# A hybrid decoder layer: dummy products at the start, copies of x moved, a bank and two products reordered

## The chip, the cores and the metric

The kernel runs on one core of a Trainium2 chip. The core has a matrix engine (TensorE, PE in the profile, with its weight loads as PEld), a vector engine (VectorE, DVE), a scalar engine (ScalarE, ACT), a general engine (GpSimd, POOL) and a synchronising engine (SyncE, SP) that here mainly issues DMAs. Each engine has its own queue of instructions, and they wait for each other by semaphores. The metric is the device time of one execution in microseconds; lower is better.

## What is computed

One layer of a decoder with 1024 positions and width 1024, in float32: a normalisation, one wide projection, two groups of heads side by side (differential softmax attention and chunked gated linear attention, GLA), an output projection, a second normalisation and the residual. Cut to what matters:

```python
def hybrid_layer(x, layer_idx, pre_g, post_g, w_in, w_gk_up, b_gk, ...):
    h = rms_norm(x, pre_g)
    z = jnp.einsum('bsd,de->bse', h, w_in)          # 1024 x 1024 by 1024 x 7184
    qa, ka, va, ga, qb, kb, vb, gb, gk_low = split_columns(z)
    ...
    oa = diff_attention(qa, ka, va, lam)            # 8 heads, causal
    oa = rms_norm(oa, subln_g) * (1.0 - lam_init)
    oa = oa * jax.nn.silu(ga)
    gk = jnp.einsum('bsr,re->bse', gk_low, w_gk_up) + b_gk
    log_a = jax.nn.log_sigmoid(gk) / 16.0
    ob = gla_chunked(qb, kb, vb, log_a)             # 4 heads
    ob = rms_norm(ob, gla_g) * jax.nn.silu(gb)
    y = jnp.einsum('bse,ed->bsd', jnp.concatenate([oa, ob], axis=-1), w_out)
    return x + rms_norm(y, post_g)
```

## The kernel before

Each float32 matrix product is made of three products in a reduced format: an operand is split into a high part (a cast, on ACT) and a low part (operand minus high part, on DVE), and high by high, high by low and low by high are added up in PSUM. All matmuls are issued at line 117 (`mm`) and all transposes at line 120 (`tr`), in the program's order on PE.

**The projection** is done by a seven-product scheme of the Strassen-Winograd kind over halves of positions and of the inner dimension. The columns of `w_in` are cut into units (`pairs`) of 256 columns; unit p and number n (1 to 7) name a product (p, n), which is 24 matmuls, 256 or 512 columns wide. The list `order` holds all products in the order in which PE runs them; `go(n)` issues the next n of them through `step`. Four units at the start, those for the values of GLA, are "wide" and share weights in twos: (0, n) and (1, n) use the same weight tiles. Numbers 1 and 2 are the first products of the left blocks h11 and h12, numbers 5, 6, 4 and 7 use the blocks s1, s2, h22 and s3, and number 3 uses s4.

**PSUM** has eight banks, handed out in turn from the list `free` (`take_bank`); a bank is put back by the Python code at once when its last reader is issued, so the next user waits for that reader by a semaphore. In `step`, number 1 opens a bank "x", 2 or 4 a bank "y", 5 a bank "z"; 6 and 7 add to "x" and 3 to "z". After 1, 6 and 7 ACT copies the running sum out (`snap`, line 427); `done` adds a copy to a bank on DVE (lines 403, 440) and the bank goes back.

**Weights.** `prepare(i)` makes the two weight tiles of `order[i]` ahead of its use: DVE forms differences in place where the scheme wants them (line 296), ACT casts the high part (line 315), DVE writes the low part (line 316). They lie in a ring of five buffers. The raw columns come by DMA into four buffers (`load_raw`, line 194); the first ten products use weights that are loaded early (`load_early`, line 236) for units 2, 3 and 4. The early tiles of unit 4 (128 wide) lie where one early tile of unit 2 was, so that their load waits until that one has been used.

**The start.** The first four tiles of x (128 positions each) are loaded, squared with a running sum on ACT (line 491), turned into a factor by `rstd` (lines 1480 to 1490) and scaled on DVE, first half, and POOL, second half (line 482). `first(0)` transposes the first half of the columns into four banks; `put` writes the blocks h11 (high on ACT, line 521, low on DVE, line 522). The product (0, 1) follows, then `first(1)` for h12, two more products, the normalisation of the tiles 4 to 7 in twos, one more product, and then four `blocks(j)`, with a product behind each. `blocks(j)` transposes two pieces of the other positions into two banks and makes h22, s1, s2 and s3 from them: evictions on ACT (lines 562 and 521), sums on DVE (lines 522, 565, 568, 569), and casts and low parts (lines 547 and 548). The block s4 follows (line 625).

**The low-rank part** of the gate (`low_rank`) loads small weights, splits them on DVE into `wl2` and `ku` (lines 647 to 656), then runs two groups of sixteen narrow products between those of the projection.

**The order of the other engines.** A scheduler in the framework sorts the instructions of ACT, DVE, POOL and SP by a timeline of its own, except those that the kernel pins with `keep_in_program_order`. The attention, GLA and output stages behind the projection have their own hand-written merge; the diff does not touch them, apart from six copies of 512 KB from x to the output (line 1275), onto which the last stage adds for the positions 512 to 1023 and 0 to 255. They stand in the program in the attention stage; the scheduler put them early in SP's queue.

Of the kernel before, what the change touches and what calls it, by code (L numbers as in the profile page):

```python
# [31 lines left out]
def hymba_kernel(  # L32
# [20 lines left out]
    nc = tc.nc  # L53
    act, dve, pool, pe, sp = nc.scalar, nc.vector, nc.gpsimd, nc.tensor, nc.sync

# [5 lines left out]


    const = ctx.enter_context(tc.tile_pool(name="const", bufs=1))
    pre_g = const.tile([P, KT], F32, name="pre_g")
    ident = const.tile([P, P], F32, name="ident")
    make_identity(nc, ident)
    eps_t = const.tile([P, 1], F32, name="eps_t")
    pool.memset(eps_t, EPS)
    ones = const.tile([P, P], F32R, name="ones")
    pool.memset(fp(ones), 1.0)  # L70

    NZ = 512
# [50 lines left out]

    edge = ctx.enter_context(tc.tile_pool(name="edge", bufs=1, side="right"))
    pool.memset(edge.tile([P, 120], F32, name="edge"), 0.0)
    hw = ctx.enter_context(tc.tile_pool(name="hw", bufs=1, side="right", reuse_waits="tile"))
    hpool_cm = tc.tile_pool(name="hpool", bufs=1, side="right")
# [89 lines left out]
    i = order.index((1, 4))  # L217
    order[i : i + 2] = order[i + 1], order[i]

    order += [(y, 1), (y, 2), (y - 1, 3), (y, 5), (z, 1), (z, 2), (z, 5), (y, 6), (z, 6), (y, 4)]  # L220
    order += [(y, 7), (z, 4), (z, 7), (y, 3), (z, 3)]
    LEAD = 8
    ws, ws_wide, early = {}, {}, {}

# [13 lines left out]
    def prepare(i):  # L238

        if i >= len(order) or i in ws:  # L240
            return
        if i < 4:

            act_ins, dve_ins = normed[0][:2]
            with tc.issue_after(act_ins.ins), tc.issue_after(dve_ins.ins):
                make_weights(i)
        else:
            make_weights(i)
# [70 lines left out]
    LEFT = {1: "h11", 2: "h12", 3: "s4", 4: "h22", 5: "s1", 6: "s2", 7: "s3"}  # L319
    NRING = 5  # L320

    def multiply(i, ps, start):
# [97 lines left out]
    def step(i):  # L420
# [22 lines left out]
        if n == 1:  # L443
            snap("s1", ps)
        elif n == 2:
            done(0, 0, ps, b["s1"])
            free.append(b["iy"])
        elif n == 6:
            snap("s2", ps)
        elif n == 7:  # L450
            snap("s3", ps)
            free.append(b["ix"])
            done(1, 1, b["z"], b["s3"])
            done(1, 0, b["y"], b["s3"])
            free.append(b["iy"])
        elif n == 3:
            done(0, 1, ps, b["s2"])
            free.append(b["iz"])
# [24 lines left out]

    norms, normed = {}, []

    def norm_x(*sts):
        n = len(sts)
        ssq = const.tile([P, 4, n], F32, tag=f"ssq{sts[0]}", name="ssq", bufs=1)
        for i, st in enumerate(sts):
            junk = hw.tile([P, D], F32, tag=("s2_hi0", "s2_lo0")[st % 2], name="junk")  # L490
            ins = act.activation(
                junk, xs[st], AF.Square, scale=D**-0.5, accum_out=ssq[:, 0, i : i + 1]
            )
            if n == 1:
                tc.keep_in_program_order(ins)
        pin = tc.keep_in_program_order if n == 1 else None
        normed[:] = [rstd(nc, ssq[:, :, :n], ssq[:, 0, :n], eps_t, pin)]
        for i, st in enumerate(sts):
            norms[st] = ssq[:, 1, i : i + 1]
            if n == 1:  # L500
                pin(scale_x(st, cols(0), dve))
            else:
# [9 lines left out]
    load_early(2)  # L512
    load_early(4)
    for st in range(4):
        norm_x(st)
# [13 lines left out]
    def first(h):  # L529

        ps = [take_bank([P, 512], "xT") for _ in range(HB)]
        for i in range(4):
            for j in range(HB):
                k = h * HB + j
                tr(ps[j][0][:, i * P : (i + 1) * P], xs[i][:, k * P : (k + 1) * P])
        hi, lo = H[("h11", "h12")[h]]
        for j in range(HB):
            put(ps[j][0], h * HB + j, (hi, lo), j)
            if h:
                act.activation(f1[h][:, j], ps[j][0], AF.Copy, scale=pre_g[:, h * HB + j : h * HB + j + 1])  # L540
# [39 lines left out]
    def wo_step(n):  # L580
# [8 lines left out]
        if n in (2, 4) and wo_todo:  # L589
# [3 lines left out]
            wo_open.append((e, dh, raw))  # L593

    def go(n):
        for _ in range(n):
            i = made[0]
            if i == len(order):
                return
# [8 lines left out]

    prepare(0)
    first(0)  # L610
    for i in range(1, 4):
        prepare(i)
    go(1)
    first(1)
    go(2)
    norm_x(4, 5)
    norm_x(6, 7)
    go(1)
    for j in range(HB):
        blocks(j)  # L620
        go(1)
    go(2)
# [11 lines left out]
    def low_rank():  # L634
# [21 lines left out]
        dve.tensor_tensor(up[96 : 96 + R], gk_up, fp(up[0:R]), ALU.subtract)  # L656
        go(2)
        for half in range(2):
# [51 lines left out]

    go(6)
    sp.dma_start(bgk, b_gk[0].rearrange("(t p) -> p t", p=P))
    low_rank()
# [5 lines left out]

    sp.dma_start(sub_g, attn_subln_g[0].rearrange("(p o) -> p o", o=1))  # L720
    dve.tensor_scalar(sub_g, sub_g, 1.0 - LAM_INIT, None, ALU.mult)
    sp.dma_start(gla_g, gla_norm_g[0].rearrange("(t p) -> p t", p=P))
    lam4 = t_c("lam4").rearrange("p (a b) -> p a b", b=128)[:, :, :64]
# [535 lines left out]
    def out_early():  # L1259
# [12 lines left out]
        for st in range(1, NT - 1):  # L1272
            part, nxt = nxt, mix(st + 1)
            rows = slice(ENDS[st - 1] * P, ENDS[st - 1] * P + P)
            sp.dma_start(out[0, rows, :], x[0, rows, :])
            for dh in range(2):
# [91 lines left out]

    LAST, ENDS = 2, [4, 5, 6, 7, 0, 1, 2, 3]

# [155 lines left out]
```

## Time and profile before

| | |
|---|---|
| time, median of 3 runs | 979.69 us (978.42 to 980.46) |
| the profiled execution | 979.08 us |
| its span, first to last instruction | 977.4 us |
| granted TensorE clock, mean over the span | 0.999 |
| DMA traffic | 220.45 MB, mean 226 GB/s |
| first matmul work | 7.21 us |
| the six copies of x, issued by SP from | 20.46 us |

The profile lists instructions by line of the kernel, engine, operation and tile. A row of the timeline begins with the start and the duration in us, then engine, line, operation, the tile written and those read, the shape, and how many instructions are merged (x16); in square brackets stands how long the engine had been idle before and what ended that. Matmuls are pipelined: the duration of one row reaches a little into the next. In the list of waits, a row has the waiting engine, tile and line, what it waited for, and us in total, number of waits, longest wait. In the chain of waits, a row has start, duration and what held the end of the execution at that time. In the list of DMA issues, the last figure is the median time in us from issue to landing.

### The profile page before, as it was taken

The page shows a single profiled execution, that of the slowest core. Times are in us where ns is not written, and L with a number is a line of the kernel's source. Part 1 is how long each engine was busy: PE and PEld are TensorE (multiplying, and loading weights), DVE is VectorE, ACT ScalarE, POOL GpSimd, SP SyncE. Part 2 cuts the span into 40 slices and gives each one's busy share as a digit, 9 for nine tenths or more (in the row PEclk, how much of TensorE's full clock was granted, in tenths as well). Part 3 has the DMA queues.
Part 4 walks back from the last instruction along what each step waited for, and adds up shares of the span by engine and source line. Part 5 has one row for each costly group of instructions (what it writes and reads, how often), then busy time and mean ns, then how long its engine had stood idle before and what let it go on. Part 6 is the DMA issues. An engine that isn't in the chain of part 4 may idle for free.

```text
span 977.4 us, 15766 instructions
## 1 busy us (share of the span) xinstructions
PE 956.7 (98%) x5338; PEld 830.4 (85%) x5338; DVE 735.4 (75%) x1452; ACT 600.5 (61%) x1164; POOL 142.9 (15%) x158
## 2 busy tenths in 40 slices
PE   5999999999999999999999999999999999999997
PEld 5998988888889998999888888878888888888785
DVE  6887597789866667686786876487888888898554
ACT  8742455487357455454665775366776687887773
POOL 4300000000000010000200002121322222443321
PEclk9999999999999999999999999999999999999999
DMA  9432446656774868897987866987656669994677
GB/s 345 151 110 91 139 135 205 231 179 225 238 247 162 264 187 286 254 294 229 293 259 243 273 202 191 407 269 272 197 186 228 240 199 344 340 294 105 151 208 147
DMA packets 152593, 220.45 MB, mean 226 GB/s; under 512 B 17104, under 2 KB 83664, under 8 KB 152416
## 3 DMA queue, kind: packets, MB, share of 16 engines
q1 hardware_dynamic: 146176, 203.71, 64.1%
q0 software_dynamic: 6336, 15.73, 7.0%
q8 instruction: 42, 0.69, 0.3%
q14 instruction: 39, 0.32, 0.1%
HBM read 133.93 MB, written 88.60 MB: 228 GB/s over the span
## 4 chain that ended last, share of the span: by engine, by line
PE 95%; DVE 2%; ACT 1%; DMA 1%; issue 1%; POOL 0%; SPq 0%; DVEq 0%; ACTq 0%; POOLq 0%
PE x L117 24%; PE y L117 15%; PE z L117 15%; PE ypart L117 13%; PE sc L117 7%; PE po L117 5%; PE yps L117 4%; PE wtr L120 3%; PE gpo L117 3%; PE kv L117 1%; PE gkl_ps L117 1%; PE pa L117 1%; DMA x<-in_x_dram 1%; PE xT L120 1%; DVE s_lo L548 0%
## 5 line engine op out<-in xcount | busy, mean ns | idle before, releaser
L315 ACT CAST w<-w_raw 128x512 fp32r<-128x512 f32 (+1 forms) x164 | 112.4, 688 | 94.7 <-PE y L117 44.1
L316 DVE TENSOR_TENSOR w<-w_raw,w 128x512 fp32r<-128x512 f32 (+1 forms) x164 | 126.7, 774 | 50.1 <-ACT w L315 43.3
L1049 ACT ACTIVATE p<-p,stt 128x896 f32<-128x896 f32 (+7 forms) x128 | 99.3, 777 | 36.7 <-DVE stt L1039 33.9
L427 ACT COPY s<-x 128x512 f32<-128x512 f32 x84 | 49.1, 585 | 84.4 <-PE x L117 84.3
L775 POOL TENSOR_SCALAR_AFFINE_SELECT gan<-gan 128x512 f32<-128x512 f32 x8 | 16.5, 2060 | 485.4 <-ACT gan L774 449.8
L296 DVE TENSOR_TENSOR w_raw<-w_raw 128x512 f32<-128x512 f32 (+1 forms) x96 | 75.9, 791 | 13.9 <-DMA w_raw<-in_w_in_dram 12.6
L1039 DVE CUSTOM_DVE_ANT_0 p<-sc,maskt 128x512 f32<-128x512 f32 (+3 forms) x128 | 74.3, 585 | 14.5 <-PE sc L117 13.3
L117 PE MATMUL ypart<-wo_hi,m_hi 128*128 128x512 f32 x192 | 79.5, 414 | 0.1
L117 PE MATMUL y<-h_hi,w 128*128 128x512 f32 x320 | 79.6, 391 | 0.0
L117 PE MATMUL z<-s_hi,w 128*128 128x512 f32 x320 | 79.6, 391 | 0.0
L117 PE MATMUL x<-s_hi,w 128*128 128x512 f32 x320 | 79.6, 391 | 0.0
L1055 POOL TENSOR_SCALAR p<-p,stt,lam 128x1024 f32<-128x1024 f32 (+3 forms) x64 | 56.2, 879 | 146.9 <-DVE stt L1054 141.9
L117 PE MATMUL ypart<-wo_hi,m_lo 128*128 128x512 f32 x192 | 75.5, 393 | 0.0
L117 PE MATMUL ypart<-wo_lo,m_hi 128*128 128x512 f32 x192 | 75.4, 393 | 0.0
L117 PE MATMUL sc<-k,q 128*128 128x512 f32 (+1 forms) x192 | 69.0, 363 | 1.3 <-DVE stt L1039 1.2
L117 PEld LDWEIGHTS x<-s_hi,w 128*128 128x128 f32 x320 | 59.7, 188 | 12.2
L117 PEld LDWEIGHTS y<-h_hi,w 128*128 128x128 f32 x320 | 59.6, 188 | 12.2
L117 PEld LDWEIGHTS z<-s_hi,w 128*128 128x128 f32 x320 | 59.5, 188 | 12.0
L117 PE MATMUL sc<-ks,q 128*128 128x512 f32 (+1 forms) x192 | 66.1, 347 | 0.0
L1097 ACT CAST wt_hi<-wtr 128x512 fp32r<-128x512 f32 (+1 forms) x80 | 42.7, 534 | 24.6 <-PE wtr L120 23.8
L1098 DVE TENSOR_TENSOR wt_lo<-wtr,wt_hi 128x512 fp32r<-128x512 f32 (+1 forms) x80 | 50.7, 633 | 8.6 <-ACT wt_hi L1097 8.0
L1058 DVE SCALAR_TENSOR_TENSOR p<-p,stt,p 128x1024 f32<-128x1024 f32 (+3 forms) x64 | 52.1, 814 | 4.1 <-POOL p L1055 3.9
(226 smaller groups left out, 2247.7 us busy)
## 6 DMA issues: line engine op xcount, KB each, us to landing
w_raw<-in_w_in_dram SPq DMA_DIRECT2D x56, 512.0 KB, 4.7
wo_raw<-in_w_out_dram SPq DMA_DIRECT2D x32, 256.0 KB, 3.0
wo_d<-wo_hi SPq DMA_DIRECT2D x32, 256.0 KB, 2.8
wo_d<-wo_raw SPq DMA_DIRECT2D x32, 256.0 KB, 3.8
q<-q_d SPq DMA_DIRECT2D x32, 256.0 KB, 4.7
k<-k_d SPq DMA_DIRECT2D x32, 256.0 KB, 5.7
ks<-k_d SPq DMA_DIRECT2D x64, 128.0 KB, 6.2
v<-v_d SPq DMA_DIRECT2D x16, 512.0 KB, 7.0
```

Of the source, the lines that this page charges most:

```text
L117: tc.keep_in_program_order(pe.matmul(*a, **k))
L120: tc.keep_in_program_order(pe.transpose(dst, src, ident))
L296: dve.tensor_tensor(dst, a, b, ALU.subtract)
L315: act.copy(w[0], src)
L316: dve.tensor_tensor(w[1], src, fp(w[0]), ALU.subtract)
L427: act.copy(b[k], ps)
L1039: ins = dve.tensor_tensor_reduce(p[:, a:e], sc[:, : e - a], maskt[:, NZ + P - (e - a) :] if last else maskt[:, : e - a], 1.0, 3e38 if i == ...
L1049: act.activation(p[:, :n], p[:, :n], AF.Exp, bias=st[:, m : m + 1], scale=-1.0, accum_out=st[:, 2 + m : 3 + m],)
L1055: pool.tensor_scalar(p1[:, :n], p1[:, :n], st[:, 5:6], lam, ALU.mult, ALU.mult)
L1058: dve.scalar_tensor_tensor(p0[:, :n], p0[:, :n], st[:, 4:5], p1[:, :n], ALU.mult, ALU.subtract)
L1097: act.copy(hi[:, :n], pt[:, :n])
L1098: dve.tensor_tensor(lo[:, :n], pt[:, :n], fp(hi[:, :n]), ALU.subtract)
```

## The change

- **Dummy products.** A tile `idle` of zeros is made on POOL, the tile `ones` and another memset are moved ahead of the identity. `spin(n)` issues n matmuls of 512 columns, `ones` by `idle`, which are added up in one tile in a bank that is free at the time; the result is read by nobody. 14 are put ahead of the transposes of `first(0)`, then 3, 7, 3 and 4 behind the transposes of its four tiles.
- **Copies of x.** The six copies leave the attention stage and are issued, pinned, ahead of the products with index 20, 24, 28, 32, 36 and 40 of `order`.
- **An early bank.** Ahead of the product behind the last `blocks(j)`, which is (3, 2), the second bank in the free list is moved to its front.
- **Two products' order.** (1, 4) is moved two places back instead of one, so (1, 7) comes before it; the sum that needs both 4 and 7 is taken behind the later of them.
- **The low-rank preparation** starts one product earlier (`go(5)` and `go(3)` in place of `go(6)` and `go(2)`), its matmuls stay in place.
- **Pinned order.** ACT, DVE and POOL are wrapped in a class that pins every instruction issued while a flag is set: from the first normalisation to the end of the second `put`. Within this stretch the weights of the first four products are now prepared ahead of `first(0)`, the normalisation of the tiles 4 to 7 and the product (0, 1) stand ahead of `first(1)`, and the weights with index 4 to 10 are made only behind the last pinned instructions. Three small loads are pinned where they stand in the program, later than the scheduler had put them.

In the built program the instructions of each engine differ in order up to about the second decay computation of the projection; behind that they stand as before. PE has 31 more matmuls.

```diff
-    act, dve, pool, pe, sp = nc.scalar, nc.vector, nc.gpsimd, nc.tensor, nc.sync
+    pe, sp = nc.tensor, nc.sync
+    pinned = [False]
+
+    class Queue:
...
+        def __getattr__(self, name):
+            op = getattr(self.engine, name)
+
+            def run(*a, **k):
+                ins = op(*a, **k)
+                if pinned[0]:
+                    tc.keep_in_program_order(ins)
+                    self.last = ins.ins
+                return ins
+
+            return run
+
+    act, dve, pool = Queue(nc.scalar), Queue(nc.vector), Queue(nc.gpsimd)
...
+    ones = const.tile([P, P], F32R, name="ones")
+    pool.memset(fp(ones), 1.0)
+    idle = hw.tile([P, 512], F32R, tag="s1_hi0", name="idle")
+    pool.memset(fp(idle), 0.0)
+    pool.memset(edge.tile([P, 120], F32, name="edge"), 0.0)
...
     i = order.index((1, 4))
-    order[i : i + 2] = order[i + 1], order[i]
+    order[i : i + 3] = order[i + 1], order[i + 2], order[i]
...
+    ENDS = [4, 5, 6, 7, 0, 1, 2, 3]
+    COPIES = range(20, 44, 4)
...
-        if i < 4:
-
-            act_ins, dve_ins = normed[0][:2]
-            with tc.issue_after(act_ins.ins), tc.issue_after(dve_ins.ins):
+        if 4 <= i <= n_early:
+            with tc.issue_after(act.last), tc.issue_after(dve.last):
                 make_weights(i)
...
+    spins = []
+
+    def spin(n):
+
+        if not spins:
+            spins.append(bank(free[-1], [P, 512], "spin"))
+        for i in range(n):
+            mm(spins[0], ones, idle, start=(i == 0), stop=(i == n - 1))
...
             done(1, 1, b["z"], b["s3"])
-            done(1, 0, b["y"], b["s3"])
-            free.append(b["iy"])
+        if n in (4, 7):
+            b.setdefault("both", []).append(n)
+            if len(b["both"]) == 2:
+                done(1, 0, b["y"], b["s3"])
+                free.append(b["iy"])
...
+    pinned[0] = True
     for st in range(4):
         norm_x(st)
...
         ps = [take_bank([P, 512], "xT") for _ in range(HB)]
+        if not h:
+            spin(14)
         for i in range(4):
             for j in range(HB):
                 k = h * HB + j
                 tr(ps[j][0][:, i * P : (i + 1) * P], xs[i][:, k * P : (k + 1) * P])
+            if not h:
+                spin((3, 7, 3, 4)[i])
         hi, lo = H[("h11", "h12")[h]]
         for j in range(HB):
             put(ps[j][0], h * HB + j, (hi, lo), j)
+        pinned[0] = not h
+        for j in range(HB):
...
+    def copy_x(st):
+
+        rows = slice(st * P, st * P + P)
+        tc.keep_in_program_order(sp.dma_start(out[0, rows, :], x[0, rows, :]))
+
     def go(n):
         for _ in range(n):
             i = made[0]
+            if i in COPIES:
+                copy_x(ENDS[COPIES.index(i)])
...
-    prepare(0)
+    for i in range(4):
+        prepare(i)
     first(0)
-    for i in range(1, 4):
-        prepare(i)
-    go(1)
-    first(1)
-    go(2)
     norm_x(4, 5)
     norm_x(6, 7)
     go(1)
+    first(1)
+    go(3)
     for j in range(HB):
         blocks(j)
+        if j == HB - 1:
+
+            free.insert(0, free.pop(1))
         go(1)
...
-        go(2)
+        go(3)
         for half in range(2):
             cs = cols(half)
             ps, i = take_bank([P, 512], "gkl_ps")
...
-    go(6)
-    sp.dma_start(bgk, b_gk[0].rearrange("(t p) -> p t", p=P))
+    go(5)
+    tc.keep_in_program_order(sp.dma_start(bgk, b_gk[0].rearrange("(t p) -> p t", p=P)))
     low_rank()
...
-            rows = slice(ENDS[st - 1] * P, ENDS[st - 1] * P + P)
-            sp.dma_start(out[0, rows, :], x[0, rows, :])
```

## What is predicted

> **What bounds the kernel now.** I read the busy shares first, then what TensorE (PE) waited for, then windows by stage, then the chain of waits between 40 and 80 us, where the diff puts its hands.
>
> ```profile
> PE 956.7 (98%) x5338; PEld 830.4 (85%) x5338; DVE 735.4 (75%) x1452; ACT 600.5 (61%) x1164; POOL 142.9 (15%) x158
> ...
> PE y L117 <- ACT s L427: 0.7, 1, 0.7
> ...
> 20.20:23.00 2.80, 2.80 (x27) 2.80 (x26) 2.80 (x4) 2.56 (x9) 1.96 (x1) 1.00 1.27 393
> 30.00:45.00 15.00, 13.68 (x117) 13.47 (x116) 13.52 (x22) 11.65 (x20) 2.74 (x5) 1.00 0.37 118
> 45.00:60.00 15.00, 14.90 (x103) 13.74 (x102) 15.00 (x23) 7.09 (x10) 0.00 (x0) 1.00 0.13 35
> 60.00:120.00 60.00, 59.32 (x441) 55.09 (x441) 39.48 (x58) 20.19 (x30) 0.00 (x0) 1.00 0.42 125
> 120.00:640.00 520.00, 519.89 (x2855) 452.99 (x2854) 385.40 (x611) 295.00 (x512) 25.87 (x25) 1.00 0.73 238
> ...
> 43.98 2.15 PE L117 MATMUL y<-w,h_hi 128*128 128x256 f32 x16 [1.32 <-DVE s L565]
> ```
>
> PE is the bound: from 120 to 640 us it idles 0.11 us. (In a window's row stand busy time and count of PE, PEld, DVE, ACT and POOL, then granted clock, DMA share and GB/s.) What a rearrangement can win lies ahead of 120 us: the start, one wait of 1.32 us for DVE, one of 0.7 us for ACT. But from 45 to 60 us DVE is busy 15.00 of 15 us too, and the chain shows what that means:
>
> ```profile
> 43.84 0.60 DVE s_lo L548
> ...
> 46.24 0.66 DVE h_lo L522
> ...
> 48.76 1.13 DVE w L316
> ...
> 58.09 1.23 DVE w L316
> ...
> 59.37 5.06 PE x L117 x40
> 64.44 2.88 PE y L117 x24
> 67.32 2.89 PE x L117 x24
> ...
> 70.87 3.14 PE y L117 x24
> ```
>
> From 43.84 us to 59.32 the end is set by DVE, back to back: 0.66 us per 512-wide operation on PSUM, 0.60 per 512-wide tensor_tensor, 1.13 per 1024-wide one. PE meets it twice, at 43.98 us and in the middle of product (0,6), whose second half starts at 59.37, when the low part of its weights is written. What is won ahead of 59 us counts only as far as DVE gets there sooner.
>
> **The change, part by part.** *The dummies.*
>
> ```profile
> 1.12 0.64 POOL L74 MEMSET maskt<- 128x640 f32 x1
> 12.71 1.11 PE L120 MATMUL xT<-ident,x 128*128 128x128 f32 x4 [0.49 <-DVE x L482]
> 14.41 4.24 PE L117 MATMUL x<-w,h_hi 128*128 128x256 f32 x16 [0.58 <-ACT h_hi L521]
> 20.01 1.91 PE L120 MATMUL xT<-ident,x 128*128 128x128 f32 x16
> 21.67 2.16 PE L117 MATMUL x<-w,h_hi 128*128 128x256 f32 x16
> 27.51 2.08 PE L117 MATMUL y<-w,h_hi 128*128 128x256 f32 x16
> ...
> 13.68 2.42 ACT L521 ACTIVATE h_hi<-xT,pre_g 128x512 fp32r<-128x512 f32 x4
> 15.35 2.71 DVE L522 SCALAR_TENSOR_TENSOR h_lo<-xT,pre_g,h_hi 128x512 fp32r<-128x512 f32 x4
> 15.97 1.07 ACT L491 ACTIVATE junk<-xt 128x1024 f32<-128x1024 f32 x1
> 19.09 0.30 ACT L1480 ACTIVATE ssq<-ssq,eps_t 128x2 f32<-128x2 f32 x1
> 19.14 1.88 DVE L296 TENSOR_TENSOR w_raw<-w_raw 128x1024 f32<-128x1024 f32 x1 [0.42 <-DMA w_raw<-in_w_in_dram]
> 20.31 0.20 ACT L1481 ACTIVATE ssq<-ssq 128x2 f32<-128x2 f32 x1
> 20.41 0.58 ACT L427 COPY s<-x 128x512 f32<-128x512 f32 x1
> 21.62 0.69 ACT L521 ACTIVATE h_hi<-xT,pre_g 128x512 fp32r<-128x512 f32 x1 [0.21 <-PE xT L120]
> 26.36 1.36 DVE L316 TENSOR_TENSOR w<-w_early,w 128x1024 fp32r<-128x1024 f32 x1
> ...
> 72.20 0.40 DVE L653 CAST ku<-gk_up 16x512 fp32r<-16x512 f32 x1
> ```
>
> Sixteen equal matmuls take 4.24 us at 14.41 and 2.16 at 21.67, though the granted clock reads 1.00 throughout: PE starts at about half pace. The 31 added matmuls of 512 columns cost some 0.24 us warm (2.88 us over 24 of half the width) and 0.48 cold. The first 14 start when the two memsets ahead of them on POOL are done, near 1.7 us (the 640-wide one took 0.64), and end by 8.4 at the latest; the batches of 3, 7 and 3 fill the gaps in which PE waits for the rows of x; the last 4, behind the transposes that start at 12.71, end near 14.1, ahead of 14.41. They cost nothing as long as the first product waits for ACT; with that cover gone, the last 4 cost their 1 us. Warm, they free the first product, which is then held by its operands: h_hi comes one piece every 0.6 us, the last piece of h_lo at 15.35 + 2.71 = 18.06. It ends near 18.4, not at 20.01: 1.6 us won.
>
> *The normalisation pinned.* ACT now runs all four squares, both logarithms and exponentials and the copy ahead of the second h_hi, in program order. From the rows: squares from 15.97, the first pair done at 18.2, logarithm and exponential 0.5, the next pair at 20.9, again 0.5, the copy at 21.4, h_hi from 22.0 with pieces at 22.7, 23.3, 23.9 and 24.4. Before, they came from 21.62. PE reaches that product at 22.95 (18.4 + 1.66 of transposes + 2.88), waits for the last piece and leaves at 26.65 (two thirds, 1.92 us, lie behind that piece), where it left at 27.51. Of the 1.6 us, 0.86 are left.
>
> *DVE's list up to the early bank.* Product (3,2) now takes a bank freed by gv_st, the 27th operation from the start of the second h_lo in the changed order: 10 on PSUM (6.6 us), 13 tensor_tensors of 512 (7.8) and 4 of 1024, two of them beside POOL's work (1.28 apart, from the 1.36 us row) and two not, together 4.8. That is 19.2 us from 22.75, plus about 0.8 of hand-overs with ACT (a single one of 0.51 is quoted below). gv_st ends at 42.8, the product starts near 42.95 instead of 43.98; PE would be ready at about 41. The wait stays because two 1024-wide subtractions, done before in the gaps ahead of 23.4 us (the first is the 1.88 us row), now stand behind h_lo.
>
> *On to 59 us.* Up to the low weights of (0,6) follow 16 tensor_tensors (9.6), 2 PSUM operations (1.3), 4 of 1024 (4.5) and, new here since the low-rank preparation moved ahead, two casts of 0.40: 16.2 us, end near 59.1. Before: 59.32. So all edits ahead of 59 us are together worth 0.1 to 0.2 us.
>
> *The two products' order.* (1,4) takes the bank that the copy of (0,7) frees; with (1,7) between, that copy has 2.88 us to finish. (0,7) ends at 70.20 and (1,4) starts at 70.87, its first matmuls long (3.14 instead of 2.88): 0.9 us won. The weights of (1,4) keep their ring buffer 2.88 us longer; those behind that need it feed the first product after the low-rank products, which gives them as long. The preparation itself, earlier, is on DVE's list above and nowhere else. Sum so far: -1.0 us.
>
> *What is late next.* In ACT's new order the cast of the fifth unit's early weights (w_early, 128-wide) stands ahead of the block stage's first eviction. Its load can be issued only when DVE has consumed the tile that it overwrites, near 28.0 us, as before.
>
> ```profile
> 27.75 0.94 SPq L236 DMA_DIRECT2D w_early<-in_w_in_dram  x2
> 34.24 0.69 DVE L568 TENSOR_TENSOR h<-f1hi,h 128x512 f32<-128x512 f32 x1 [0.51 <-DVE s L565]
> 36.49 0.63 ACT L315 CAST w<-w_early 128x512 fp32r<-128x512 f32 x1
> ...
> w_early<-in_w_in_dram SPq DMA_DIRECT2D x2, 256.0 KB, 6.9
> wo_raw<-in_w_out_dram SPq DMA_DIRECT2D x32, 256.0 KB, 3.0
> gv_d<-gv_st SPq DMA_DIRECT2D x32, 128.0 KB, 2.0
> out_dram<-in_x_dram SPq DMA_DIRECT2D x6, 512.0 KB, 7.5
> 100.31 0.69 DVE L296 TENSOR_TENSOR w_raw<-w_raw 128x512 f32<-128x512 f32 x1 [3.58 <-DMA w_raw<-in_w_in_dram]
> ```
>
> Before, the cast ran at 36.49 us. Now two evictions, DVE's h_lo and s, and through them the bank, queue behind it on ACT. With a landing time L the cast starts at 28.0 + L, DVE gets its operand 1.9 us later (a cast and two evictions) and would otherwise be free for it at 32.0: it idles L - 2.1, of which 0.4 is in the 0.8 above. The cost is L - 2.5, and nothing below that. L lies between 2.0 (a write of 128 KB) and 6.9 (the same load, issued behind six 512 KB copies that are gone from there now). I take 3.0, the same size in ordinary traffic: +0.5 us. The page "DMA: Bandwidth & Descriptors" of the Trainium skill (Anatomy of one DMA) gives about 2.0 us fixed plus the bytes over 436 GB/s, an estimate of 2.6 us for this load, by which the cost would be 0.1 us; no row of before shows such a load without company.
>
> *The copies of x.* The six copies leave a stretch with a DMA share of 1.27 and go between products from 85 to 150 us, where it is 0.42 to 0.73. SP's queue puts each ahead of weight loads, most of which are issued microseconds later, when a buffer comes free. I take 0. The upper bound is one load held up for what a copy takes beyond the load's slack, 7.5 - 3.6 or so: 4 us; a gain is excluded, PE having 0.11 us of idle time there.
>
> The sum is -1.0 + 0.5 = -0.5 us. The profiled execution took 979.08 us (span 977.4, 1.7 around it), so 978.6; that execution lies 0.6 below the median of 979.69, and on the median's scale the forecast is 979.2 us. A measurement of this kernel tells about 0.2% (1.96 us) from no change, so this counts as none.
>
> **The rivals.** (1) *DVE is no wall.* Its list gets through sooner than I add up and the stalls go with the cold start: 1.6 + 1.3 + 0.9 = 3.8 us, 975.9. For it: DVE still idles 1.5 us between 30 and 45 us, and the copies that crowded its loads are gone. Against it: 15.00 of 15 us, and level cadences over 15 us of chain. It passes 0.2% when DVE reaches 59 us 1.5 us sooner than my sum. (2) *ACT stands behind the late load.* At L = 6.9 the cost is 4.4, the change +3.4, 983.1 us. It decides from L = 3.5 (break-even) and passes 0.2% at L = 5.5. For it: 6.9 us were measured for this very load. Against: its company is gone. (3) *A copy delays a weight load that PE needs*: up to +4, half of that likelier, 981 us; for it, DVE already waits 3.58 us for such a load at 100.31; against, the loads are issued well behind the copies. (4) *The dummies do not warm PE.* Then each takes 0.48 us, the last 4 end at 12.71 + 1.11 + 1.92 = 15.7 and the first product is 1.3 us late and as slow as before; with -0.9 and +0.5 about 980.6, still no change.
>
> **How the numbers follow.** Forecast and rival (4), both within 0.2%: 0.45 and 0.05, so 0.50. Rival (1), whole or in large part: 0.33. Rivals (2) and (3): 0.10 and 0.07. The forecast's own range is 978.2 (L below 2.5, DVE half a microsecond sooner) to 980.8. The 8-in-10 range reaches into most of rivals (1) and (3): 976.4 to 981.6.
>
> **What would show it.** In the changed profile: the first 16 products near 2.5 us in place of 4.24, held by h_hi; PE waiting some 0.3 us at a time near 24; the wait of (3,2) still there at 42 to 44 us, for gv_st; (0,6)'s second half at 59.1 plus what L adds; no wait near 70; ACT's cast of the 128-wide w_early behind an idle stretch that a DMA ends. If DVE idles more than 1.5 us between 25 and 55, (2) is at work; if (0,6) runs through by 58.3, (1); a PE wait between 87 and 160 us, (3).

## The result and the profile after

| | before | after |
|---|---|---|
| time, median of 22 runs | 979.32 us (978.42 to 980.84) | 981.82 us (979.41 to 983.72) |
| ratio, 95% interval | | 1.0020 (1.0013 to 1.0027) |
| the profiled execution | 979.08 us | 979.88 us |
| its span | 977.4 us | 978.2 us |

The change costs 2.5 us by the medians and 2.0 by the ratio, where 0.5 us less had been forecast, and the time lies 0.2 us above the upper end of the 8-in-10 range. The single executions spread over 4.3 us, before over 2.4. The profiled execution is one of the quicker ones, 1.9 us below the median, so its trace holds only a part of the loss.

The view of waits of TensorE after (waiting tile and line, what it waited for, us in total, number, longest; lines behind the new wrapper all read L66), and the windows that answer to those of before:

```profile
PE y L141 <- DVE gv_st L66: 2.0, 1, 2.0
PE x L141 <- DVE w L66: 1.0, 1, 1.0
PE gpo L141 <- DVE gu L66: 0.3, 1, 0.3
```

```profile
30.00:45.00 15.00, 13.02 (x111) 12.78 (x110) 14.22 (x23) 11.74 (x20) 2.73 (x5) 1.00 0.25 79
45.00:60.00 15.00, 13.95 (x96) 12.79 (x94) 14.94 (x23) 6.49 (x10) 0.00 (x0) 1.00 0.20 49
60.00:120.00 60.00, 60.00 (x446) 55.91 (x447) 39.48 (x57) 20.90 (x30) 0.00 (x0) 1.00 0.47 146
120.00:640.00 520.00, 519.60 (x2850) 452.28 (x2849) 384.56 (x611) 294.57 (x512) 26.94 (x25) 1.00 0.75 241
```

The wait near 70 us is gone (60.00 of 60 us busy). TensorE (PE) idles longer ahead of 60 us, and a wait of a kind that before did not have stands between 120 and 640 us: gpo for gu, a product of GLA for VectorE's (DVE's) state step. The timeline after, at the places of which the prediction speaks:

```profile
13.65 3.18 PE L141 MATMUL x<-w,h_hi 128*128 128x256 f32 x16
17.89 1.91 PE L144 MATMUL xT<-ident,x 128*128 128x128 f32 x16
26.48 2.06 PE L141 MATMUL y<-w,h_hi 128*128 128x256 f32 x16
28.38 0.92 SPq L259 DMA_DIRECT2D w_early<-in_w_in_dram  x2
31.33 0.62 ACT L66 CAST w<-w_early 128x512 fp32r<-128x512 f32 x1 [3.22 <-DMA w_early<-in_w_in_dram]
43.59 2.18 PE L141 MATMUL y<-w,h_hi 128*128 128x256 f32 x16 [1.98 <-DVE gv_st L66]
59.96 1.22 PE L141 MATMUL x<-w,s_hi 128*128 128x256 f32 x8 [1.05 <-DVE w L66]
129.81 1.98 PE L141 MATMUL x<-h_hi,w 128*128 128x512 f32 x8
```

The same product as in the last row, in the timeline before:

```profile
130.05 1.98 PE L117 MATMUL x<-h_hi,w 128*128 128x512 f32 x8
```

In this pair of executions the change is 0.24 us ahead at 130 us and 0.80 behind at the end. So 1.0 us goes behind the part that the change touches. Aligned by their tiles, the products keep the -0.2 up to 407 us and are 0.42 late from 411 us on; the rest goes in small steps behind that. The chain of waits (start, duration, what held the end) says what happens at 410 us. Before, it is PE alone there:

```profile
401.57 5.61 PE x L117 x36
407.18 3.57 PE gpo L117 x32
410.75 2.87 PE x L117 x24
```

After, it leaves PE and comes back at 410.23:

```profile
382.41 3.87 DMA wo_raw<-in_w_out_dram
...
402.25 6.29 DMA w_raw<-in_w_in_dram
408.56 0.04 DVE w_raw L66
...
409.70 0.49 DVE gu L66
410.23 0.94 PE gpo L141 x6
```

A load of output weights (wo_raw) lands; ACT, DVE and SP's queue of stores take 16 us; behind those stores SP issues a load of input weights (w_raw); it lands at 408.54; DVE subtracts in it, and only then makes the state step gu that the product needs. The step does not need the load. It stands behind it on DVE because the scheduler put it there, in both kernels. In the timeline of before, the same two VectorE rows and the matmul that reads gu:

```profile
407.62 1.23 DVE L296 TENSOR_TENSOR w_raw<-w_raw 128x1024 f32<-128x1024 f32 x1 [0.82 <-DMA w_raw<-in_w_in_dram]
408.76 0.48 DVE L803 SCALAR_TENSOR_TENSOR gu<-gu,dstep,kv 128x256 f32<-128x256 f32 x1
409.92 0.39 PE L117 MATMUL gpo<-gqd,gu 128*128 128x128 f32 x2
```

There the step ends at 409.24 and PE comes at 409.92: 0.7 us to spare.

One pair of traces says little about 0.24 us, though. Two traces of the kernel before and three of the changed one run the same instructions up to 400 us (e1 is the changed kernel again, e5 and e6 differ only at 410 us). The first product is done, and the product of the last rows starts, at these times in us:

| trace | first product done | product at 130 us | between |
|---|---|---|---|
| before | 20.01 | 130.05 | 110.04 |
| e6, as before up to 400 us | 19.21 | 129.24 | 110.03 |
| after | 17.89 | 129.81 | 111.92 |
| e1, the same kernel | 18.02 | 129.99 | 111.97 |
| e5, as after up to 400 us | 18.44 | 130.32 | 111.88 |

The starts spread by 0.8 and 0.55 us within the two groups; what lies between is the same within 0.1 us. The trace of before that the prediction read has the later start of the two. Over these traces the change gains 1.5 us by the first product, loses 1.9 by 130 us and is then 0.4 us late on average, not 0.24 early.

### The profile page after: what moved, and what is told of

It is laid out like the page before. It is cut to its first block, busy times and chain, and to the rows that moved or that the text cites. A ratio compares the mean times of both kernels' runs of the same rounds, so it can differ in the third digit from the quotient of the medians.

```text
span 978.2 us, 15832 instructions
## 1 busy us (share of the span) xinstructions
PE 963.6 (99%) x5369; PEld 834.2 (85%) x5369; DVE 737.9 (75%) x1452; ACT 600.7 (61%) x1164; POOL 142.8 (15%) x159
## 4 chain that ended last, share of the span: by engine, by line
PE 85%; DVE 4%; ACT 4%; DMA 3%; issue 2%; SPq 1%; POOL 0%; DVEq 0%; ACTq 0%; POOLq 0%
PE x L141 20%; PE z L141 14%; PE y L141 13%; PE ypart L141 13%; PE sc L141 7%; PE po L141 5%; PE yps L141 4%; PE wtr L144 3%; PE gpo L141 2%; PE kv L141 1%; ACT junk L66 1%; PE gkl_ps L141 1%; DMA w_raw<-in_w_in_dram 1%; DVE s_lo L66 1%; PE pa L141 1%
## 5 line engine op out<-in xcount | busy, mean ns | idle before, releaser
L66 ACT CAST w<-w_raw 128x512 fp32r<-128x512 f32 (+1 forms) x164 | 112.2, 688 | 91.8 <-PE y L141 39.9
L66 DVE TENSOR_TENSOR w<-w_raw,w 128x512 fp32r<-128x512 f32 (+1 forms) x164 | 126.6, 774 | 49.2 <-ACT w L66 43.1
L66 ACT ACTIVATE p<-p,stt 128x896 f32<-128x896 f32 (+7 forms) x128 | 99.3, 776 | 37.1 <-DVE stt L66 36.1
L66 ACT COPY s<-x 128x512 f32<-128x512 f32 x84 | 49.1, 585 | 82.1 <-PE x L141 81.7
L66 POOL TENSOR_SCALAR_AFFINE_SELECT gan<-gan 128x512 f32<-128x512 f32 x8 | 18.2, 2275 | 485.9 <-ACT gan L66 451.6
L66 DVE TENSOR_TENSOR w_raw<-w_raw 128x512 f32<-128x512 f32 (+1 forms) x96 | 75.6, 788 | 15.0 <-DMA w_raw<-in_w_in_dram 13.7
L66 DVE CUSTOM_DVE_ANT_0 p<-sc,maskt 128x512 f32<-128x512 f32 (+3 forms) x128 | 74.3, 585 | 14.6 <-PE sc L141 13.3
L66 POOL TENSOR_SCALAR p<-p,stt,lam 128x1024 f32<-128x1024 f32 (+3 forms) x64 | 56.0, 875 | 147.2 <-DVE stt L66 141.6
L141 PEld LDWEIGHTS y<-h_hi,w 128*128 128x128 f32 x320 | 59.6, 188 | 12.2
L66 ACT CAST wt_hi<-wtr 128x512 fp32r<-128x512 f32 (+1 forms) x80 | 42.8, 534 | 25.0 <-PE wtr L144 24.3
L66 DVE TENSOR_TENSOR wt_lo<-wtr,wt_hi 128x512 fp32r<-128x512 f32 (+1 forms) x80 | 50.7, 633 | 8.9 <-ACT wt_hi L66 8.2
L66 DVE SCALAR_TENSOR_TENSOR p<-p,stt,p 128x1024 f32<-128x1024 f32 (+3 forms) x64 | 52.1, 814 | 4.1 <-POOL p L66 3.8
```

The lines of the kernel that those rows point to most:

```text
L66: ins = op(*a, **k)
L141: tc.keep_in_program_order(pe.matmul(*a, **k))
```

## The experiments

Theories at the start: (A) the copies of x in mid-projection keep weights back; (B) the dummies change what the clock gate grants later; (C) late landings hold DVE and through it a product in the second half of the projection. All ratios are to the kernel before, measured in the same round on the same chip; e1 to e4, e5 to e8, e9 to e11 and e12 to e14 ran on four chips, so that ratios compare across them better than medians do. Edits are to the changed kernel unless said otherwise.

**e1: the changed kernel once more.** No edit.

> The changed kernel itself once more, for a second trace and for the spread. All theories: median 981 to 982.5 us, ratio to the kernel before 1.001 to 1.003, single executions from 979.4 to 983.7. If this trace is of a longer execution (981.5 us or more), theory A (the copies of x between 120 and 240 us keep weights back) wants a new idle of TensorE of 1 us or more between 120 and 260 us; theory B (the dummies change what the clock gate grants later) wants TensorE's granted clock below 0.998 at a place where it is 1.00 in the quick execution; theory C (a landing late in the second half of the projections holds VectorE, which holds a product) wants idle ends of 0.5 to 2 us that name DVE at 240 to 640 us.

Measured: 981.5 us (979.7 to 984.46), ratio 1.0019 (1.0009 to 1.0029). The execution with the profile took 984.46 us, so this trace holds the loss. Its chain of waits at the same place:

```profile
383.02 5.28 DMA wo_raw<-in_w_out_dram
...
404.29 6.05 DMA w_raw<-in_w_in_dram
410.36 0.04 DVE w_raw L66
...
411.50 0.48 DVE gu L66
412.03 1.57 PE gpo L141 x6
```

The load of wo_raw took 5.28 us, not 3.87; everything behind it in SP's queue is 2 us late; gu is ready at 411.98. PE's timeline, and the granted clock (third number from the end) in the windows:

```profile
412.03 0.71 PE L141 MATMUL gpo<-gqd,gu 128*128 128x128 f32 x2 [1.92 <-DVE gu L66]
413.25 3.18 PE L141 MATMUL x<-w,h_hi 128*128 128x256 f32 x16
```

```profile
412.00:414.00 2.00, 1.97 (x9) 1.97 (x10) 2.00 (x4) 0.63 (x1) 0.00 (x0) 0.54 0.51 157
414.00:416.00 2.00, 2.00 (x13) 2.00 (x12) 1.44 (x3) 1.72 (x4) 0.00 (x0) 0.61 0.61 119
```

PE idles 1.92 us, and behind the idle the clock falls to 0.54 and 0.61 for 4 us: sixteen matmuls take 3.18 us in place of 2.16. Lost there by the clock: 2 x 0.46 + 2 x 0.39 = 1.7 us, which is not made good: aligned by tiles, this trace is 0.03 us behind before's at 400 us and 3.8 behind at 415. Between 120 and 260 us there is no new idle. A has no trace here; C has, with a clock drop that neither B nor C had named, since it follows an idle and comes 400 us after the dummies.

**e2: the copies back where they were.**

```diff
-            if i in COPIES:
-                copy_x(ENDS[COPIES.index(i)])
...
+            rows = slice(ENDS[st - 1] * P, ENDS[st - 1] * P + P)
+            sp.dma_start(out[0, rows, :], x[0, rows, :])
```

> The changed kernel with the six copies of x put back where the kernel before issues them (in SP's queue at some 20 us). Theory A (copies mid-projection collide with weights): the longer executions go, median 979 to 980 us, ratio below 1.0007. Theory B (dummies and clock) and theory C (landings in the second half, whatever the copies do): median stays 981 to 982.5 us, ratio 1.001 to 1.003.

Measured: 982.2 us, ratio 1.0023 (1.0011 to 1.0034). No gain. With the copies back the scheduler also puts the late cast of w_early behind part of the block stage, so this is not the copies alone; e4 is.

**e3: no dummies.**

```diff
-        if not h:
-            spin(14)
...
-            if not h:
-                spin((3, 7, 3, 4)[i])
```

> The changed kernel without the 31 dummy products. Theory B: the longer executions go, median 979 to 980 us and the granted clock 0.998 or more in all. Theories A and C: first product up to 2 us later, of which nothing or up to 1 us reaches the end, so median 981.5 to 983 us, spread as wide as that of the changed kernel.

Measured: 980.42 us (979.34 to 981.52), ratio 1.0008 (1.0000 to 1.0017). The time lies between B's range (979 to 980) and that of A and C (981.5 to 983): a miss for all three. The mean granted clock is 0.996 or 0.997 in 6 of 11 executions, and the drop stands at 44 us, behind an idle of 2.46 us for gv_st. Without dummies the clock drops too, so B's mechanism falls. But the changed kernel is some 1.1 us quicker without its dummies (medians 980.42 and 981.5 in one round), and the trace does not say why: PE is 0.5 us later at 406 us and nothing waits at 410, so that from 411 us on the two traces lie within 0.04 us of each other. What the dummies cost stays open.

**e4: before, with the copies moved alone.** The edit is the change's own, applied to the kernel before.

> The kernel before with only the six copies of x moved to the ranks 20, 24 .. 40 of the product order. Theory A: 981 to 982 us, ratio 1.0015 to 1.003. Theories B and C: 979 to 980 us, ratio 0.9995 to 1.0007.

Measured: 979.57 us, ratio 1.0003 (0.9994 to 1.0012). A falls. In the trace this kernel is 1.27 us ahead of before at 130 us, but 1.13 of that stands at 20 us already, where it lies within the spread of the starts. It is still 1.26 ahead at 355 and waits 0.9 us for gu at 410; its span is 977.3 against 977.4. What this execution has in hand ahead of 400 us is lost there.

**e5: the state step ahead of the subtraction.** Two neighbouring DVE instructions change places; nothing else moves on any engine.

```diff
-                        dve.scalar_tensor_tensor(
+                        step_u = dve.scalar_tensor_tensor(
                             u, u1, dsteps[g][:, n + i : n + i + 1], kv[:, i], ALU.mult, ALU.add
                         )
+                        last_u[:] = [step_u.ins]
...
+        elif order[i] == (18, 5):
+            with tc.issue_after(last_u[0]):
+                make_weights(i)
```

> The changed kernel with two neighbouring VectorE instructions swapped: the last state step of the second head's second half (gu, at 409.7 us) now runs before the subtraction of a weight load (w_raw, at 408.6 us) that it stood behind, so that no product at 410 us waits for that load. Theory C (the load lands late, VectorE holds the step behind it, TensorE idles 0.3 to 2 us, and an idle near 2 us also lowers the granted clock): no wait gpo<-gu in the trace, median 978.7 to 980 us, ratio 0.9993 to 1.0007, no execution above 981.5. Rival E (the longer executions come from the idle of 2.0 us at 43 us, which lies at the edge of a clock drop, and the wait at 410 us is only one more of many): median stays at 981 us or more and the spread reaches 983.

Measured: 980.0 us (979.14 to 981.21), ratio 1.0006 (0.9997 to 1.0015). The wait is gone from the trace, the ratio is 0.0013 to 0.0014 below that of the changed kernel (some 1.3 us), and the executions spread over 2.1 us in place of 4.3. C holds. A part of E seems to hold as well: the mean clock is 0.996 or 0.997 in 6 of the 11 executions, and the trace shows the drop at 43 us. Timeline and windows of e5:

```profile
44.03 3.40 PE L141 MATMUL y<-w,h_hi 128*128 128x256 f32 x16 [1.86 <-DVE gv_st L66]
...
48.50 2.00 PE L141 MATMUL x<-h_hi,w 128*128 128x512 f32 x8
...
59.72 2.08 PE L141 MATMUL x<-w,s_hi 128*128 128x256 f32 x16
```

```profile
44.00:46.00 2.00, 1.97 (x11) 1.97 (x12) 2.00 (x4) 0.39 (x1) 0.00 (x0) 0.63 0.38 131
46.00:48.00 2.00, 2.00 (x11) 2.00 (x11) 2.00 (x4) 0.62 (x1) 0.00 (x0) 0.51 0.00 0
```

The same idle was 1.98 us in the changed kernel's trace, with no drop behind it. Here 1.86 us is followed by 3.6 us or so at half pace, and the product takes 3.40 us in place of 2.18. The product (0,6) at 59.72 then runs through, where the changed kernel's waits 1.05 us in its middle for DVE's weights: PE comes so much later that the weights are ready. And the 6 executions with the lower clock are no longer than the other 5 (medians 979.72 and 980.12).

**e6: before, with the same swap.**

> The kernel before with the same swap of the two VectorE instructions. Theory C: before's profiled execution had no wait there, so only its longer executions can gain: median 978.4 to 979.3 us, ratio 0.9988 to 1.0, spread under 2 us. Rival E: no change, 979.2 to 979.8 us, ratio 0.9997 to 1.0003.

Measured: 978.4 us (977.63 to 980.37), ratio 0.9992 (0.9983 to 1.0002). The median is as C expected, the spread of 2.7 us is not, and the interval just takes in no change. So the swap takes 0.0008 out of before's ratio too. Before must wait at 410 us in some executions: in e6's own trace the subtraction starts at 408.77, 1.15 us later than in before's, and the step behind it would have been too late for PE at 409.66. The fair comparison of the change without that wait is therefore e5 against e6, on one chip: ratios of 1.0006 and 0.9992, medians of 980.0 and 978.4. The change still costs 1.4 to 1.6 us there.

**e7: before, with the copies moved and the swap.**

> The kernel before with the copies of x moved (e4) and the swap. e4 was 1.26 us ahead of before at 355 us and lost it at 410 us. Theory C: that now reaches the end: median 977.8 to 978.6 us, ratio 0.9983 to 0.9992. Rival E: as e4, 979.3 to 979.9 us, ratio 1.0 to 1.0005.

Measured: 978.46 us (978.0 to 979.46), ratio 0.9991 (0.9982 to 1.0000), as C expected. Of all kernels here it has the least spread, and its trace no clock drop ahead of the tail. It is below both kernels, but not below e6 (978.4), so the copies add nothing that shows.

**e8: e7 with the order of the two products.**

> e7 with the order of the two products too, which should take the wait of 0.7 us for ACT's s out of the stretch near 70 us. Theory C: median 977.2 to 978.2 us, ratio 0.9978 to 0.9988, and 0.5 us or more ahead of e7 in the trace at 130 us. Rival E: 979 to 980 us, ratio 0.9995 to 1.0005.

Measured: 981.69 us, ratio 1.0021 (1.0013 to 1.0030): a miss. The wait near 70 us goes, and the next one is behind it, in the timeline of e8:

```profile
78.05 3.13 PE L117 MATMUL gkl_ps<-h_hi,wl 128*64 128x512 f32 x8 [2.21 <-DVE wl L667]
```

The low-rank products wait 2.21 us for their weights, and the clock drops behind it. In this kernel the reordering needs the earlier low-rank preparation that the change brings along with it (e11 has it, and the wait is gone).

**e9: w_early(4) in a buffer of its own**, which its load need not wait for. PE, DVE and ACT run the same instructions in the same order.

```diff
-            r = kp.tile([P, 2, HB, P], F32, tag="ks0", name="w_early")
+            r = hw.tile([P, 2, HB, P], F32, tag="s1_hi1", name="w_early")
```

> The changed kernel with w_early(4) in a buffer of its own, so that its load needn't wait for w_early(2)'s readers and lands by 24 us in place of 31.3; PE, DVE and ACT run the same instructions in the same order. Theory F (the idle of 2.0 us before y(3,2) at 43 us comes from that landing and lies at the edge of a clock drop that costs some 1.6 us more): idle there under 1 us, no clock below 0.95 between 20 and 400 us, 1.5 to 3 us ahead of the changed kernel at 130 us. As the wait at 410 us is still there (theory C), most of that is lost at 410 us, with an idle of 1.5 to 3.5 us before gpo and a clock drop: median 980 to 982 us, ratio 1.0005 to 1.0025. Rival G (VectorE's queue is the limit up to 60 us, so the landing doesn't matter): less than 0.7 us ahead at 130 us.

Measured: 980.15 us (978.63 to 984.48), ratio 1.0010 (0.9999 to 1.0021). The cast now runs at 29.33 us, the idle at 43 us falls from 1.98 to 1.14, there is no drop, and the product at 129.81 starts at 128.79. That is 1.02 us ahead of the changed kernel, of which 0.22 stand at 27 us already, ahead of the late load: some 0.8 us is what the landing costs. F named an idle under 1 us and a lead of 1.5, G a lead below 0.7; neither is met. At the end of the trace nothing of it is left (span 978.4), and single executions still reach 984.48: the wait at 410 us is still there (0.3 us in this trace).

**e10: e9 with the swap.**

> e9 with the swap of e5. Theories C and F together: no wait gpo<-gu, no clock drop before the tail, what is ahead at 130 us reaches the end: median 976.5 to 978.5 us, ratio 0.997 to 0.9992, spread under 2 us. Rival G: 979.5 to 980.3 us, as e5.

Measured: 979.51 us (978.35 to 981.14), ratio 0.9997 (0.9988 to 1.0006). No clock drop, no wait for gu; but the median is 1 us above what C and F together expected and the spread of 2.8 us above their 2; the time is what G expected.

**e11: before, with copies, order, low-rank preparation, swap and buffer.**

> The kernel before with the copies moved, the two products' order, the earlier low-rank preparation, the swap of e5 and the buffer of e9: the change without dummies, early bank and written-out order. Theories C and F: the wait wl of 2.2 us that e8 showed at 78 us is gone, nothing else takes its place: median 976.5 to 978.2 us, ratio 0.997 to 0.9988. Rival G: 978 to 978.8 us.

Measured: 979.94 us, ratio 1.0002 (0.9993 to 1.0011): a miss for both. The wait for wl is gone; in its place stand two of 1.58 us (w) and 1.39 us (s_lo) at 59 and 62 us.

**e12: e5 with the idle at 43 us filled.**

```diff
+        if order[i] == (3, 2):
+            d = bank(free[0], [P, 512], "spin")
+            for k in range(5):
+                mm(d[:, :P], ones, ones, start=(k == 0), stop=(k == 4))
         multiply(i, ps, n not in (6, 7, 3))
```

> e5 with five dummy products of 128x128 right before the product at 43 us that waits for gv_st; they write a bank that is free some 0.6 us sooner than the product's own, so the idle of 1.9 us is cut in two and the product itself starts as before. Nothing else moves. Theory F (an idle near 2 us lowers the granted clock for some 3.4 us, which costs 1.5 us): no clock below 0.95 at 43 to 48 us in the trace, the stretch 0.9 to 1.5 us shorter than in e5's trace, median 978.4 to 979.4 us, ratio 0.9985 to 1.0. Rival K (the clock drop follows from something else, and dummies only add work): drop still there, median 980 us or more, ratio 1.0005 to 1.0015.

Measured: 979.68 us (979.17 to 981.15), ratio 1.0001 (0.9992 to 1.0010); the mean clock is 0.998 or 0.999 in all 11 executions. The time is 0.3 us above F's range and 0.3 below K's. Timeline and windows of e12:

```profile
43.22 0.74 PE L141 MATMUL spin<-ones 128*128 128x128 f32 x5 [1.53 <-DVE s L66]
43.80 2.12 PE L141 MATMUL y<-w,h_hi 128*128 128x256 f32 x16
...
46.71 2.00 PE L141 MATMUL x<-h_hi,w 128*128 128x512 f32 x8
...
60.09 1.21 PE L141 MATMUL x<-w,s_hi 128*128 128x256 f32 x8 [1.04 <-DVE w L66]
```

```profile
44.00:46.00 2.00, 2.00 (x19) 2.00 (x19) 2.00 (x5) 0.08 (x1) 0.00 (x0) 1.00 0.38 131
46.00:48.00 2.00, 2.00 (x14) 1.78 (x13) 2.00 (x5) 0.62 (x1) 0.00 (x0) 1.00 0.00 0
```

The product starts as long after the idle began as in e5, the clock stays at 1.00, and the product behind it starts 2.91 us after it (46.71) and not 4.47 us (48.50 in e5). So the drop needs the idle in one piece, and it takes 1.5 us at this place. But only there: at 60.09 e12 waits 1.04 us for DVE's weights, which e5 does not. At the product of 130 us e12 is 0.37 us ahead of e5 (129.95 and 130.32), of which 0.23 stand at 43 us, ahead of the drop. Some 0.1 us of the 1.5 is left, because DVE and not PE sets the time at 60 us. On the medians the difference is 0.3 us and 0.0005 in the ratio, within both intervals, and nothing shows that it comes from the clock.

**e13: e5 without the early bank.**

```diff
-        if j == HB - 1:
-
-            free.insert(0, free.pop(1))
```

> e5 without the early bank: the product at 43 us takes a bank whose last reader on VectorE is s, 0.66 us ahead of gv_st. Theory J (the early bank hands over the bank that comes free last): idle at 43 us falls from 1.9 to 1.2 to 1.4 us, no clock drop there, median 978.4 to 979.5 us, ratio 0.9985 to 1.0. Rival (the early bank saves more later than it costs here): a new wait of 0.5 us or more between 44 and 80 us, median 979.8 to 981 us, ratio 1.0003 to 1.0015.

Measured: 981.21 us, ratio 1.0016 (1.0008 to 1.0025). The idle at 43 us falls to 1.44 (J had 1.2 to 1.4), and no clock drop follows; but in e13's timeline two waits come behind it:

```profile
42.99 2.14 PE L141 MATMUL y<-w,h_hi 128*128 128x256 f32 x16 [1.44 <-DVE s L66]
59.85 1.22 PE L141 MATMUL x<-w,s_hi 128*128 128x256 f32 x8 [1.57 <-DVE w L66]
63.17 0.50 PE L141 MATMUL x<-w,s_lo 128*128 128x256 f32 x2 [1.38 <-DVE s_lo L66]
```

The rival holds: the early bank is worth more than it costs. (On DVE the scheduler moves some neighbouring operations by a place or a few with it, so this is not the bank alone; e11 and e14, which lack the early bank too, show the same two waits.)

**e14: e13 with the buffer of e9.**

> e13 with w_early(4) in a buffer of its own (e9). If the waits add up: idle at 43 us 0.3 to 0.7 us, 0.6 us ahead of e10 at 130 us, median 978 to 979 us, ratio 0.998 to 0.9995. If VectorE's queue gives it back at 60 us (wait x<-w above 1.5 us): median 979 to 980 us, ratio 0.9992 to 1.0005.

Measured: 980.41 us, ratio 1.0007 (0.9998 to 1.0016). Idle 0.63 us at 43 us, and the same two waits of 1.56 and 1.38 at 59 and 62: DVE's queue gives it back. The time is 0.4 us above the range named for that.

## Why the prediction was wrong

The steps up to 130 us, against the trace of after:

- *Dummies*: the first product is done at 17.89 (18.4 predicted), 2.1 us sooner than in before's trace, in place of 1.6. The dummies are the smaller part of it: e3, whose last transposes start at the same 12.18 us, has it done at 18.47 without them, so they give 0.6 us there, and the rest comes from h_hi, which starts at 12.91 in place of 13.68, and from where the starts of the two executions fell. The last four dummies make way at 13.65, about when the first piece of h_hi is ready.
- *Pinned normalisation*: y(1,2) starts at 26.48, 1.03 us sooner than before; predicted were 0.86.
- *DVE's list and the early bank*: the list began at 23.36 and not at 22.75. The second h_hi came 1.0 us sooner than predicted (20.98, not 22.0), but h_lo stood behind four tiny DVE operations that waited for POOL (last section), a wait that the prediction put at nothing. Product (3,2) starts at 43.59, predicted 42.95 + 0.5; (0,6)'s second half at 59.96, predicted 59.1 + 0.5. DVE is the wall there, and rival (1) did not come: it is busy 14.94 of 15 us from 45 to 60.
- *The late load*: landing time 31.33 - 28.38 = 2.95 us, where I took 3.0. The estimate of 2.6 from the page "DMA: Bandwidth & Descriptors" of the Trainium skill (Anatomy of one DMA) was nearly as close, though the page fits that sum for transfers issued by GpSimd and SP issued this one. The price of the landing was too small: e9 shows some 0.8 us, not 0.5.
- *The two products' order*: no wait near 70, 0.83 us won of the 0.9 predicted (from 59.96 - 59.37 = +0.59 to -0.24 at 130).
- *Copies*: no wait between 85 and 160 us, and e4 is no slower. Rival (3) fell.

In this pair of traces the sum of -0.5 us comes out at -0.24, but by luck of the pair: over the five traces of the table it is +0.4. The stretch from the first product to 59 us, predicted at 41.2 us (18.4 to 59.6), took 42.1 in after and in e1: it was the term that came out too small, by 0.9 us, and DVE's late start and the landing are what the traces show of it.

The step that failed outright is one that the prediction did not write out: that its sum at 130 us reaches the end. It read "from 120 to 640 us it idles 0.11 us" as PE being the only bound there. The row showed no idle; it did not show how much room there was. At 410 us it was 0.7 us, behind a chain of loads, stores and DVE work that before's chain of waits does not name at all because PE was just the later of the two. In the changed kernel PE comes 0.14 us sooner and the load lands 0.9 us later: 0.6 us lost in the trace of after, 3.8 us in that of e1 (2.1 by the wait, from 409.92 to 412.03, and 1.7 by the clock). The swap alone takes 0.0013 out of the ratio (e1 to e5), some 1.3 us. It takes 0.0008 out of before's (e6), so the wait accounts for some 0.5 us of the difference between the two kernels; the other 1.4 to 1.6 us stand without it (e5 against e6).

The clock drop behind the wait of (3,2) is not a second cause. The wait was foreseen at its place and nearly at its length, and the drop that sometimes follows it was not; but DVE's wall at 60 us takes up all but some 0.1 us of it (e5 against e12), and the executions of e5 that have it are no longer than the others.

What stays open is most of the difference: with the wait gone from both kernels the change still costs 1.4 to 1.6 us. The 0.4 us at 130 us are a part of it; no trace here places the rest. In e1, e2, e13 and e14 a wait of 0.16 to 0.75 us for ACT's s stands near 525 us that no trace of before, e4, e6, e7, e8 or e11 has; it was not followed. Neither was it found why the changed kernel is 1.1 us quicker without its dummies (e3), nor why wo_raw's load takes 3.9 us in one execution and 5.3 in another. e6 and e7 are the quickest kernels here, though the interval of each reaches 1.

## What to carry to other kernels

An engine that shows no idle time in a window has shown nothing about its slack: before summing a gain to the end, look for every operand of the bound engine whose producer finishes just ahead of it, and for what that producer queues behind. A state step that stands on an in-order engine behind an operation on a fresh load turns that load's landing time into a wait for TensorE; putting the step first cost nothing here (e6). A wait of TensorE near 2 us is to be priced with the clock drop that can follow it, but only where TensorE is the bound: at 410 us the drop's 1.7 us stayed lost, at 43 us DVE's wall took up nearly all of its 1.5. And the start of one execution differs from the next by 0.8 us here, so a gain of half a microsecond is read from several traces or not at all.

## What the hardware showed unexpectedly

**The clock drops behind idles that are shorter than expected.** Ahead of a drop to about 0.5 stood idles of 1.86 us (e5), 1.92 (e1), 2.21 (e8), 2.38 (e2) and 2.46 (e3); none followed 1.98 us in the changed kernel or 2.02 at the same place in e1, and none any of 1.6 us or less. In the windows the drop lasts 3 to 4 us. The Trainium skill ("TensorE: Matmul & The Clock Gate", Part 1) has a window of 3.4 us and says that it runs freely, which would fit that an idle of 1.86 drops and a longer one does not. Its rule to allow no idle above about 3 us (section "Why this matters for your kernels") is too lax here: 1.86 us was enough.

**Tiny DVE operations wait for POOL.** Four 128x2 operations on DVE take over 1 us each in the changed kernel. Timeline after:

```profile
15.61 5.04 POOL L66 TENSOR_TENSOR f1hi<-h_hi,h_lo 128x512 f32<-128x512 f32 x4 [2.95 <-DVE h_lo L66]
18.29 1.13 DVE L1531 TENSOR_TENSOR ssq<-ssq 128x2 f32<-128x2 f32 x1
19.45 1.21 DVE L1532 TENSOR_TENSOR ssq<-ssq 128x2 f32<-128x2 f32 x1
20.70 0.16 DVE L1533 SCALAR_TENSOR_TENSOR ssq<-ssq 128x2 f32<-128x2 f32 x1
...
20.98 2.43 ACT L66 ACTIVATE h_hi<-xT,pre_g 128x512 fp32r<-128x512 f32 x4
...
23.36 0.74 DVE L66 SCALAR_TENSOR_TENSOR h_lo<-xT,pre_g,h_hi 128x512 fp32r<-128x512 f32 x1
```

The second ends at 20.66, when POOL's four f1hi end (15.61 + 5.04 = 20.65); the next operation takes 0.16. The page "SBUF — State Buffer" of the Trainium skill (Terms, shared port pair) says that the two engines share a pair of ports as a lock, held for the whole instruction, and that the loser blocks fully; the rows agree. The pinned order puts two such pairs ahead of h_lo, which starts at 23.36 though the first of the four pieces of h_hi is made by about 21.6.
